# Masked copies in blocks of 32 keys by 32 queries in a chunked gated linear scan: one instruction for all partitions instead of four

## The chip, the cores and the metric

The kernel runs on one core of one Trainium2 chip. The metric is the device time of one execution in microseconds (us). Engines are named as in the profile: PE is TensorE (PEld its weight loads), DVE is VectorE, ACT is ScalarE, POOL is GpSimd, SP issues DMAs. Each engine takes its own instructions strictly in order and waits on semaphores for the others.

## The reference

One inference step of a decoder layer on 256 prompt tokens and 8 x 4 sample tokens, width 2048: a SwiGLU block, a mixer, a second SwiGLU block, each with RMSNorms around it. The mixer projects the tokens, runs two groups of gated recurrences (GLA: 4 heads with value width 256; HGRN2: 8 heads with value width 128; key width 128 in both), normalises and gates their outputs and projects back.

```python
def gated_linear_scan(q, k, v, log_a, s0):
    # S_t = diag(exp(log_a_t)) S_{t-1} + k_t^T v_t ;  o_t = q_t S_t
    ...
    def step(s, inp):
        qi, ki, vi, gi = inp                      # one chunk of c tokens
        cum = jnp.cumsum(gi, axis=2)
        diff = cum[:, :, :, None, :] - cum[:, :, None, :, :]
        decay = jnp.where(causal, jnp.exp(jnp.where(causal, diff, 0.0)), 0.0)
        scores = jnp.sum(qi[:, :, :, None, :] * ki[:, :, None, :, :] * decay, axis=-1)
        o = (jnp.einsum('bhts,bhsv->bhtv', scores, vi)
             + jnp.einsum('bhtd,bhdv->bhtv', qi * jnp.exp(cum), s))
        last = cum[:, :, -1:, :]
        s_new = (jnp.exp(last[:, :, 0, :])[..., None] * s
                 + jnp.einsum('bhsd,bhsv->bhdv', ki * jnp.exp(last - cum), vi))
        return s_new, o
```

What matters here are the `scores`: for each query token t and each key token s not after it, the sum over 128 features of q_t times k_s times the decay from s to t. For s = t there is no decay, and the score is the plain sum of q_t k_t.

## The kernel before

**Products.** Nearly all time goes to dense products. An activation tile holds 128 features by 288 tokens (256 prompt, 32 sample). Weights arrive as float32 tiles of 128x1024 and are split into a high part `wh` (ACT, L96) and a low part `wl` (DVE, L97). `block` multiplies each with the activations' two parts in three products per 128x128 piece, on L548 (high by high), L549 (low activations by high weights) and L550 (high activations by low weights). Four split weight tiles are held ahead. The names of the products are `gate`, `up`, `out` (the SwiGLU blocks), `qk`, `v`, `hfq`, `hi`, `gate` and `mo` (the mixer).

**Scans.** Six scans, one per pair of heads (two GLA, then four HGRN), run while `block` works on the next projection: `scan` is a generator, and at each `tick` in `block` it issues its next piece. A scan handles two heads (index a) and two halves of 128 prompt tokens (index i). The scores of one half are gathered in `Dg`, 128 keys by i, a and 128 queries (`Dflat` is the same with i and a joined); those of the sample tokens are in `Ds`. Later `out` multiplies `Dg` and `Ds` with the values.

**Levels.** A pair of tokens s < t belongs to level lv if lv is the highest bit in which they differ: then s lies in the left and t in the right half of a block of 2h tokens, h = 2^lv. At each level `update(lv)` (L1022 and L1025, with the decay products F of L1027) multiplies Q and k with decays, so that one product of k and Q gives that level's scores. In the order of the steps:

- `score01` (L959, L975, L979) gives levels 0 and 1 and s = t; `score23` (L959) levels 2 and 3, from the copies R of L1032, L1037 and L1038; `score(lv)` (L959 for level 4, L1069 for 5 and 6, L1055 for 7) the others.
- For levels 0 to 4 `quarters` computes, for 32 keys each, only the queries of the same 32 tokens: 16 products per call, of 32 keys by 16, 32 or 48 columns. The four groups of 32 keys write the four groups of 32 partitions of PSUM.
- Of these scores only some belong to the level. `put_masked` copies them into the diagonal blocks of `Dg` under a mask `mk` (COPY_PREDICATED on DVE, L968), in four instructions, one for each 32 partitions, since each group of partitions has its own columns in `Dg`. Levels 0 and 1 take eight such instructions, levels 2 and 3 take twelve (level 3 has a near and a far variant). Level 4 needs no mask: ACT copies it in four instructions (L1080). Levels 5 to 7 are copied by ACT (L1086, L1076).
- The sum for s = t is made by a product of the elementwise q k (`own`, in `rp`, L1093, scaled by 128) with a matrix of ones/128. It is split in two reduced-precision parts, `oh` (ACT, L1095) and `ol` (DVE, L1097), and so takes two products of 128x288 (L975). Every partition then holds all sums, and two masked copies with an identity mask (L995) put them on the diagonal of `Dg`; five more (L1001, L1009) fill `Ds`.

The order in which the instructions of each engine stand is not only that of the program: a planner in the framework moves them by its own estimates of when each can start. Each engine then executes its list in that order, whatever the real times are.

**Setup.** `setup` loads the masks as integers into `mi32`, a buffer that `Q` of the first scan uses next (L1096), and POOL casts them to bytes in `mk` (L842).

Of the kernel before, what the change touches and what calls it, by code (L numbers as in the profile page):

```python
# [9 lines left out]
F32 = mybir.dt.float32  # L10
# [115 lines left out]
def trunk_kernel(ctx, tc, x_prompt, x_sample, state_gla, state_hgrn, norm_gains, f1_in, f1_out, f2_in, f2_out,  # L126
# [649 lines left out]
    def mixer(pn, border):  # L776
        with ExitStack() as mx:
# [15 lines left out]
            mk = cst.tile([P, 576], U8, name="mk")  # L793
# [27 lines left out]
            def setup():  # L821
# [20 lines left out]
                G.tensor_copy(mk, mi32)  # L842
# [67 lines left out]
            def scan(d, Vt, V32, Vs, gla, ytile0, s0, sp_out, ss_out):  # L910
# [34 lines left out]
                oh = sp[0].tile([P, T], F32R, name="oh", tag="bd")  # L945
                ol = sp[0].tile([P, T], F32R, name="ol", tag="bd")
# [15 lines left out]
                def put_masked(src, h, m):  # L962

                    for b in range(4):
                        r = slice(b * TS, (b + 1) * TS)
                        dst = Dflat[r, :, r].rearrange("p j (n two k) -> p j n two k", two=2, k=h)[:, :, :, 1, :]
                        mv = mk[r, m * 64 + b * 16:m * 64 + (b + 1) * 16].rearrange("p (n k) -> p n k", k=h)
                        V.copy_predicated(dst, mv.unsqueeze(1).broadcast_to(dst.shape),  # L968
                                          src[r].rearrange("p j (n k) -> p j n k", k=h))

                def score01():

                    ps, po = auxtile("sc01"), auxtile("sc_o")
                    for i, part in enumerate((oh, ol)):
                        PE.matmul(po[:, 0:T], ones[128], part, start=i == 0, stop=i == 1, skip_group_check=True)  # L975
                    quarters(ps, lambda i, a, b: R[:, a, :, i * 64 + b * 16:i * 64 + (b + 1) * 16])
                    for a in range(2):
                        c = T + a * TS
                        PE.matmul(po[0:TS, c:c + TS], k[:, a, TP:T], R[:, a, :, P:P + TS // 2],  # L979
                                  start=False, stop=True, skip_group_check=True)  # L980
                    return ps, po

                def put01(ps, po):
                    def eye(n, m):
                        return mk[0:n, 448:448 + 2 * m].rearrange("p (n two) -> p n two", two=2)[:, :, 0]

                    def odd():
                        for lv in range(2):
                            put_masked(ps[:, 0:P].rearrange("p (j l c) -> p j l c", j=4, l=2)[:, :, lv], 1 << lv, lv)

                    def even():
                        v = Dflat.rearrange("p (i a) (n two) -> p i a n two", a=2, two=2)
                        ov = po[:, 0:T].rearrange("p (a c) -> p a c", a=2)
                        for i in range(2):
                            V.copy_predicated(v[:, i, :, :, 0], eye(P, 64).unsqueeze(1).broadcast_to([P, 2, 64]),  # L995
                                              ov[:, :, i * 64:(i + 1) * 64])

                    def sampled():
                        sv = Ds[0:TS].rearrange("p a (n two) -> p a n two", two=2)
                        ov = po[:, 0:T].rearrange("p (a c) -> p a c", a=2)  # L1000
                        V.copy_predicated(sv[:, :, :, 0], eye(TS, 16).unsqueeze(1).broadcast_to([TS, 2, 16]),  # L1001
                                          ov[0:TS, :, P:])
                        for lv in range(2):
                            h = 1 << lv
                            m = mk[:, lv * 64:(lv + 1) * 64]
                            dst = Ds[0:TS].rearrange("p a (n two k) -> p a n two k", two=2, k=h)[:, :, :, 1, :]
                            for a in range(2):
                                c = T + a * TS + lv * 16
                                V.copy_predicated(dst[:, a], m[0:TS, 0:16].rearrange("p (n k) -> p n k", k=h),  # L1009
                                                  po[0:TS, c:c + 16].rearrange("p (n k) -> p n k", k=h))  # L1010

                    return [odd, even, sampled]
# [60 lines left out]
                def put(lv, ps):  # L1073
# [3 lines left out]
                    elif h == 16:  # L1077

                        for b in range(0, P, TS):
                            S.activation(Dflat[b:b + h, :, b + h:b + TS],  # L1080
                                         ps[b:b + h, 0:64].rearrange("p (j c) -> p j c", j=4), AF.Copy)
# [9 lines left out]
                for step in range(LEVELS + 1):  # L1091
                    if step == 0:
                        V.scalar_tensor_tensor(own.unsqueeze(3), halves(q, 1, False), 128.0, halves(k, 1, False),  # L1093
                                               op0=ALU.mult, op1=ALU.mult)
                        S.activation(oh, rp, AF.Copy)  # L1095
                        V.tensor_tensor(Q, q, d["f"], op=ALU.mult)  # L1096
                        V.tensor_tensor(ol, rp, oh.bitcast(F32), op=ALU.subtract)  # L1097
# [28 lines left out]
                    if 3 <= step < LEVELS - 1:  # L1126
# [4 lines left out]
                        elif step == 4:  # L1131
                            sampled()
                            put23(*pss.pop(3))
                        else:
                            put(step - 1, pss.pop(step - 1))
# [387 lines left out]
```

## Time and profile before

| what | value |
|---|---|
| median of 3 runs | 2266.98 us (2266.93 to 2267.67) |
| the profiled execution, its own time | 2267.07 us |
| its span, first to last instruction | 2265.0 us |
| PE, PEld busy in the span | 2244.5 us, 2227.3 us |
| DVE, ACT, POOL busy in the span | 1409.0 us, 1022.7 us, 134.9 us |
| granted TensorE clock | 0.998 |
| scan stage | 923 us to 1246 us of the span |

The page gives each engine's busy share of the span; the windows view gives it for a stretch of time. The view of waits lists who stood idle and whose instruction released it, with total, count and longest in us. The groups show line, engine, operation, output<-inputs, shapes and count, then busy time, mean ns of one, and the idle time before them with its releaser. The timeline lists instructions by start and duration, runs of equal ones merged.

### The profile page before, as it was taken

Reading aid. Unit: us, or ns where it says so; the run is one execution under the profiler, and the core shown is the slowest. Engines: PE = TensorE matmul, PEld = TensorE weight load, DVE = VectorE, ACT = ScalarE, POOL = GpSimd, SP = SyncE. Lnnn points to the kernel's source line nnn. Section 1 sums busy time; section 2 is a strip of 40 time slices with the busy share of each in tenths; the row PEclk is TensorE's granted clock in tenths of the full one; section 3 lists DMA queues with packets and bytes.
Section 4 is the critical chain, followed back from the end, with each engine's and each line's share of the span. In section 5 each row is a group of like instructions: output and inputs, shape, how many; then the busy total and the mean of one; then the engine's idle time right before and its main releaser. Section 6 shows DMA issues by size and latency. Waiting matters only on the chain. (4 is left out here: it accounts for less than half of the span.)

```text
span 2265.0 us, 43259 instructions
## 1 busy us (share of the span) xinstructions
PE 2244.5 (99%) x17760; PEld 2227.3 (98%) x17760; DVE 1409.0 (62%) x2359; ACT 1022.7 (45%) x1581; POOL 134.9 (6%) x241
## 2 busy tenths in 40 slices
PE   9999999999999999999999999999999999999998
PEld 9999999999999999999999999999999999999998
DVE  6545545554555468888889754954555455545546
ACT  6443333333334346555656654644333333333344
POOL 2000000000000001011000000440000000000005
PEclk9999999999999999999999999999999999999999
DMA  6555555555555554566555554565555555555545
GB/s 213 171 165 167 168 167 163 165 167 168 167 164 182 167 168 140 168 187 189 163 167 177 164 186 150 168 190 165 164 167 167 168 164 164 165 168 168 164 164 156
DMA packets 225605, 382.49 MB, mean 169 GB/s; under 512 B 20242, under 2 KB 60224, under 8 KB 225408
## 3 DMA queue, kind: packets, MB, share of 16 engines
q1 hardware_dynamic: 214736, 365.15, 50.6%
q0 software_dynamic: 8496, 14.41, 2.4%
q8 instruction: 139, 2.28, 0.4%
q10 hardware_dynamic: 2176, 0.18, 0.1%
q14 instruction: 58, 0.48, 0.1%
HBM read 363.75 MB, written 11.80 MB: 166 GB/s over the span
## 5 line engine op out<-in xcount | busy, mean ns | idle before, releaser
L97 DVE TENSOR_TENSOR wl<-raw,wh 128x1024 fp32r<-128x1024 f32 (+1 forms) x674 | 821.7, 1220 | 615.3 <-ACT wh L96 612.7
L96 ACT ACTIVATE wh<-raw 128x1024 fp32r<-128x1024 f32 (+1 forms) x674 | 711.5, 1057 | 1018.9 <-PE gate L549 313.7
L548 PE MATMUL gate<-xh,wh 128*128 128x288 f32 x1660 | 488.4, 296 | 0.6 <-ACT xh L254 0.6
L550 PE MATMUL gate<-xh,wl 128*128 128x288 f32 x1660 | 488.5, 295 | 0.4 <-DVE wl L97 0.4
L549 PE MATMUL gate<-xl,wh 128*128 128x288 f32 x1660 | 485.7, 295 | 0.6 <-DVE xl L255 0.6
L549 PE MATMUL out<-hl,wh 128*128 128x288 f32 x1408 | 415.7, 295 | 0.0
L550 PE MATMUL up<-xh,wl 128*128 128x288 f32 x1408 | 415.0, 295 | 0.0
L550 PE MATMUL out<-hh,wl 128*128 128x288 f32 x1408 | 415.0, 295 | 0.0
L548 PE MATMUL up<-xh,wh 128*128 128x288 f32 x1408 | 414.9, 295 | 0.0
L549 PE MATMUL up<-xl,wh 128*128 128x288 f32 x1408 | 414.6, 294 | 0.0
L548 PE MATMUL out<-hh,wh 128*128 128x288 f32 x1408 | 413.7, 294 | 0.0
L548 PEld LDWEIGHTS gate<-xh,wh 128*128 128x128 f32 x1660 | 310.9, 188 | 1.9 <-ACT xh L254 1.0
L550 PEld LDWEIGHTS gate<-xh,wl 128*128 128x128 f32 x1660 | 311.3, 188 | 1.1 <-DVE wl L97 0.8
L549 PEld LDWEIGHTS gate<-xl,wh 128*128 128x128 f32 x1660 | 310.4, 188 | 1.2 <-DVE xl L255 0.8
L550 PEld LDWEIGHTS out<-hh,wl 128*128 128x128 f32 x1408 | 264.7, 188 | 0.0
L548 PEld LDWEIGHTS out<-hh,wh 128*128 128x128 f32 x1408 | 264.6, 188 | 0.0
L549 PEld LDWEIGHTS out<-hl,wh 128*128 128x128 f32 x1408 | 264.4, 188 | 0.0
L548 PEld LDWEIGHTS up<-xh,wh 128*128 128x128 f32 x1408 | 264.1, 188 | 0.3
L549 PEld LDWEIGHTS up<-xl,wh 128*128 128x128 f32 x1408 | 264.2, 188 | 0.1
L550 PEld LDWEIGHTS up<-xh,wl 128*128 128x128 f32 x1408 | 264.2, 188 | 0.0
L706 DVE TENSOR_TENSOR y<-out,y 128x288 f32<-128x288 f32 x288 | 121.2, 452 | 101.3 <-PE out L550 98.3
L548 PE MATMUL hfq<-xh,wh 128*128 128x288 f32 x256 | 77.6, 304 | 0.0
(376 smaller groups left out, 2518.9 us busy)
## 6 DMA issues: line engine op xcount, KB each, us to landing
raw<-in_ffn_w_in_dram SPq DMA_DIRECT2D x351, 512.0 KB, 3.5
raw<-in_ffn_w_out_dram SPq DMA_DIRECT2D x176, 512.0 KB, 3.5
raw<-in_mix_w_in_dram SPq DMA_DIRECT2D x64, 512.0 KB, 3.8
raw<-in_mix_w_in_dram SPq DMA_DIRECT2D x96, 256.0 KB, 3.1
raw<-in_mix_w_out_dram SPq DMA_DIRECT2D x32, 512.0 KB, 3.6
out_dram<-s POOLq DMA_DIRECT2D x32, 256.0 KB, 2.8
s<-in_state_gla_dram SPq DMA_DIRECT2D x16, 256.0 KB, 4.2
s<-in_state_hgrn_dram SPq DMA_DIRECT2D x16, 256.0 KB, 4.2
```

Of the source, the lines that this page charges most:

```text
L96: i1 = self.nc.scalar.activation(h[:, c], raw[:, c], AF.Copy).ins
L97: i2 = self.nc.vector.tensor_tensor(l[:, c], raw[:, c], h[:, c].bitcast(F32), op=ALU.subtract).ins
L548: yield lambda: PE.matmul(dst, w[0][:, c:c + P], parts[0], start=start, stop=False)
L549: yield lambda: PE.matmul(dst, w[0][:, c:c + P], parts[1], start=False, stop=False)
L550: yield lambda: PE.matmul(dst, w[1][:, c:c + P], parts[0], start=False, stop=stop)
L706: V.tensor_tensor(y[k], ps, y[k], op=ALU.add)
```

## The change

The masked copies of levels 0 to 3 no longer write `Dg`. A new tile `Db` holds, for each of the 128 keys, only the 32 queries of its own block, so that all 128 partitions have the same columns, and one COPY_PREDICATED does the work of four. Level 4 goes the same way, on DVE under its mask. A new function `place` copies the four blocks of `Db` to the diagonal of `Dg` on ACT, one step after level 4. The sum for s = t is computed in blocks like the other scores: float32 products with a 128x32 matrix of ones, eight for the prompt and two for the sample, in place of the two of 128x288; `oh` and `ol` go, and the factor 128. `Ds` is filled by three copies instead of five. The masks are cast in eight pieces by POOL, which also fills `Db` with zeros and the ones.

```diff
-            mk = cst.tile([P, 576], U8, name="mk")
+            mk = cst.tile([P, 8, 16], U8, name="mk")
+            one32 = cst.tile([P, TS], F32, name="one32")
+            Db = cst.tile([P, 4, TS], F32, name="Db")
...
-                G.tensor_copy(mk, mi32)
+                G.memset(one32, 1.0)
+                G.memset(Db, 0.0)
+                for b in range(4):
+                    r = slice(b * TS, (b + 1) * TS)
+                    G.tensor_copy(mk[r, 0:7], mi32[r, 0:448].rearrange("p (l c) -> p l c", c=64)[:, :, b * 16:(b + 1) * 16])
+                    G.tensor_copy(mk[r, 7], mi32[r, 448 + b * TS:448 + (b + 1) * TS]
+                                  .rearrange("p (n two) -> p n two", two=2)[:, :, 0])
...
                 def put_masked(src, h, m):
+                    dst = Db.rearrange("p j (n two k) -> p j n two k", two=2, k=h)[:, :, :, 1, :]
+                    mv = mk[:, m, :].rearrange("p (n k) -> p n k", k=h)
+                    V.copy_predicated(dst, mv.unsqueeze(1).broadcast_to(dst.shape),
+                                      src.rearrange("p j (n k) -> p j n k", k=h))
+
+                def place():
                     for b in range(4):
                         r = slice(b * TS, (b + 1) * TS)
-                        dst = Dflat[r, :, r].rearrange("p j (n two k) -> p j n two k", two=2, k=h)[:, :, :, 1, :]
-                        mv = mk[r, m * 64 + b * 16:m * 64 + (b + 1) * 16].rearrange("p (n k) -> p n k", k=h)
-                        V.copy_predicated(dst, mv.unsqueeze(1).broadcast_to(dst.shape),
-                                          src[r].rearrange("p j (n k) -> p j n k", k=h))
+                        S.activation(Dflat[r, :, r], Db[r], AF.Copy)
 
                 def score01():
-                    ps, po = auxtile("sc01"), auxtile("sc_o")
-                    for i, part in enumerate((oh, ol)):
-                        PE.matmul(po[:, 0:T], ones[128], part, start=i == 0, stop=i == 1, skip_group_check=True)
+                    ps = auxtile("sc01")
                     quarters(ps, lambda i, a, b: R[:, a, :, i * 64 + b * 16:i * 64 + (b + 1) * 16])
+                    v = ps[:, P:P + 64].rearrange("p (i a c) -> p i a c", i=2, a=2)
                     for a in range(2):
-                        c = T + a * TS
-                        PE.matmul(po[0:TS, c:c + TS], k[:, a, TP:T], R[:, a, :, P:P + TS // 2],
+                        for b in range(4):
+                            PE.matmul(v[b * TS:(b + 1) * TS, :, a, :], one32,
+                                      own[:, a, 0:P].rearrange("p (i c) -> p i c", i=2)[:, :, b * 16:(b + 1) * 16],
+                                      start=False, stop=True, skip_group_check=True)
+                    for a in range(2):
+                        c = 192 + a * 16
+                        PE.matmul(ps[0:TS, c:c + 16], one32, own[:, a, P:P + 16],
                                   start=False, stop=True, skip_group_check=True)
+                        c = 224 + a * TS
+                        PE.matmul(ps[0:TS, c:c + TS], k[:, a, TP:T], R[:, a, :, P:P + TS // 2],
+                                  start=False, stop=True, skip_group_check=True)
...
+                def put01(ps):
+                    for lv in range(2):
+                        put_masked(ps[:, 0:P].rearrange("p (j l c) -> p j l c", j=4, l=2)[:, :, lv], 1 << lv, lv)
+                    dst = Db.rearrange("p j (n two) -> p j n two", two=2)[:, :, :, 0]
+                    V.copy_predicated(dst, mk[:, 7, :].unsqueeze(1).broadcast_to(dst.shape),
+                                      ps[:, P:P + 64].rearrange("p (j c) -> p j c", j=4))
...
                     elif h == 16:
-                        for b in range(0, P, TS):
-                            S.activation(Dflat[b:b + h, :, b + h:b + TS],
-                                         ps[b:b + h, 0:64].rearrange("p (j c) -> p j c", j=4), AF.Copy)
+                        put_masked(ps[:, 0:64].rearrange("p (j c) -> p j c", j=4), h, lv)
...
-                        V.scalar_tensor_tensor(own.unsqueeze(3), halves(q, 1, False), 128.0, halves(k, 1, False),
-                                               op0=ALU.mult, op1=ALU.mult)
-                        S.activation(oh, rp, AF.Copy)
+                        V.tensor_tensor(own.unsqueeze(3), halves(q, 1, False), halves(k, 1, False), op=ALU.mult)
                         V.tensor_tensor(Q, q, d["f"], op=ALU.mult)
-                        V.tensor_tensor(ol, rp, oh.bitcast(F32), op=ALU.subtract)
...
-                            odd, even, sampled = put01(*pss.pop(1))
-                            odd()
-                            even()
+                            put01(pss[1])
                         elif step == 4:
-                            sampled()
+                            put01_sample(pss.pop(1))
                             put23(*pss.pop(3))
                         else:
                             put(step - 1, pss.pop(step - 1))
+                            if step == 6:
+                                place()
```

`put01_sample` is the former `sampled` with three copies: the diagonal of `Ds`, then one for each of levels 0 and 1, both heads at once.

40 lines of the change are left out of this document (11 added, 29 removed).

## The prediction

> **What bounds the kernel now.** I read the page first, then the windows view cut at the ends of the scan stage, then what TensorE waits for inside that stage, then the timeline around the longest of those waits.
>
> ```profile
> span 2265.0 us, 43259 instructions
> PE 2244.5 (99%) x17760; PEld 2227.3 (98%) x17760; DVE 1409.0 (62%) x2359; ACT 1022.7 (45%) x1581; POOL 134.9 (6%) x241
> DVE  6545545554555468888889754954555455545546
> ```
>
> TensorE is busy 99% of the span, so the time can fall only by its work or by the 20.5 us (2265.0 - 2244.5) in which it stands still. VectorE has spare time as a whole, but slices 16 to 22 of 40, where the scans run, show eight tenths and more.
>
> ```profile
> 0.00:60.00 60.00, 57.29 (x413) 56.06 (x413) 41.53 (x72) 38.24 (x70) 15.38 (x35) 1.00 0.69 212
> 60.00:923.00 863.00, 862.80 (x6506) 861.76 (x6505) 497.03 (x724) 358.52 (x466) 12.88 (x27) 1.00 0.51 165
> 923.00:1246.00 323.00, 315.55 (x3205) 302.84 (x3204) 282.48 (x685) 189.86 (x452) 26.06 (x38) 1.00 0.60 178
> 1246.00:2265.00 1019.00, 1008.85 (x7644) 1006.69 (x7642) 587.94 (x881) 436.06 (x595) 80.58 (x141) 1.00 0.53 167
> ```
>
> The columns are length, then busy PE, PEld, DVE, ACT, POOL. Of TensorE's idle time 7.45 us (323.00 - 315.55) lies in the scan stage; the rest is the start (2.7), the end (10.2) and nearly nothing between. In the scan stage VectorE is busy 282.48 of 323 us, 87%. What ended TensorE's waits there:
>
> ```profile
> PE sc L959 <- DVE k_h L1025: 2.6, 3, 1.2
> PE sc L1069 <- DVE F L1027: 1.6, 2, 1.3
> PE hfq L550 <- DVE wl L97: 1.2, 2, 0.8
> PE sc L959 <- DVE R L1038: 1.0, 2, 0.6
> PE sc L959 <- DVE Dg L968: 0.6, 1, 0.6
> PE sc L1069 <- DVE k_h L1025: 0.3, 1, 0.3
> PE sc L959 <- DVE r L1248: 0.2, 1, 0.2
> ```
>
> Twelve waits, 7.5 us, and VectorE releases every one. Idle time starts only when the modelled tail of the last matmul has ended (matmuls start 0.13 us apart and last 0.29), so up to 0.16 us of each wait is hidden in "busy": 12 x 0.16 is 1.9 us, and removing all twelve is worth 7.5 to 9.4 us. That is the whole prize: nothing else in the change touches the bound. The longest wait shows what VectorE was doing instead:
>
> ```profile
> 1061.52 1.94 DVE L968 COPY_PREDICATED Dg<-mk,sc 32x64 f32<-32x64 uint8 x6
> 1063.94 0.74 DVE L995 COPY_PREDICATED Dg<-mk,sc_o 128x128 f32<-128x128 uint8 x2
> 1066.42 0.21 DVE L1001 COPY_PREDICATED Ds<-mk,sc_o 32x32 f32<-32x32 uint8 x1
> 1066.52 0.47 DVE L1009 COPY_PREDICATED Ds<-mk,sc_o 32x16 f32<-32x16 uint8 x4
> 1066.90 3.02 DVE L968 COPY_PREDICATED Dg<-mk,sc 32x64 f32<-32x64 uint8 x12
> 1069.94 0.43 DVE L1022 TENSOR_TENSOR Q<-Q,F 128x256 f32<-128x256 f32 x1
> 1070.29 0.42 DVE L1025 TENSOR_TENSOR k_h<-k_h,F 128x256 f32<-128x256 f32 x1
> 1070.85 0.33 PE L1069 MATMUL sc<-Q,k_h 128*32 128x32 f32 x16 [1.30 <-DVE F L1027]
> ```
>
> The level-5 scores need the updated Q and k of lines 1022 and 1025. These stood in VectorE's queue behind the twelve copies of levels 2 and 3 (3.02 us), which nobody needed yet. The next weight part, L97, queues in the same way, hence the waits on wl.
>
> **VectorE.** Per scan the old kernel has 20 copies on L968, two on L995, five on L1001 and L1009, and the subtraction L1097.
>
> ```profile
> L97 DVE TENSOR_TENSOR wl<-raw,wh 128x1024 fp32r<-128x1024 f32 x78 | 95.1, 1220 | 11.1 <-ACT wh L96 10.6
> L968 DVE COPY_PREDICATED Dg<-mk,sc 32x64 f32<-32x64 uint8 x120 | 30.4, 254 | 3.4
> L995 DVE COPY_PREDICATED Dg<-mk,sc_o 128x128 f32<-128x128 uint8 x12 | 4.4, 472 | 0.2
> L1009 DVE COPY_PREDICATED Ds<-mk,sc_o 32x16 f32<-32x16 uint8 x24 | 2.9, 180 | 0.0
> L1097 DVE TENSOR_TENSOR ol<-rp,oh 128x288 fp32r<-128x288 f32 x5 | 2.2, 450 | 0.0
> ```
>
> That is 20 x 0.254 = 5.1, plus 0.74 for the pair, 0.57 for the five (1066.42 to 1066.99 above), plus 0.45: 6.9 us. New are seven copies into Db (levels 0 and 1, the diagonal, three for levels 2 and 3, and level 4, which ScalarE did before) and three into Ds. A copy of 64 elements on all 128 partitions is not in the trace. From below: L968's 0.254, since each partition has the same 64 elements; from above: L995's 0.472 for 128 elements on 128 partitions. I take 0.254, the row with the same elements per partition. For Ds, 3 x 0.21 (L1001's size). New total 7 x 0.254 + 0.63 = 2.4 us (3.9 at the upper price). VectorE saves 4.5 us per scan (3.0 at least), 27 us over six scans, and goes from 87% to 79% busy in this stage.
>
> The Trainium skill, page "VectorE: DVE Perf Modes", section "Two Vector instructions with no wait between them", says that an instruction whose operands start in another quadrant of 32 partitions than those before it waits until every earlier one has finished. The trace agrees: the twelve L968, which step through the quadrants, lie 0.25 us apart, a full duration, while the four L1009, all in the first quadrant, lie 0.10 us apart. By this rule the new copies could overlap too, ten of them in some 1.2 us where nothing waits, and the sum below would be about 0.2 us better.
>
> What this does to the waits: ahead of the level-4 update stand, of a scan's copies, six L968 (1.94), the L995 pair (0.74) and the subtraction (0.45), and in their place comes one diagonal copy (0.25): that update can be 2.9 us earlier. Ahead of level 5 the twelve become three, 3.02 to 0.76, another 2.3: 5.1 us in all. Ahead of the level-2 and level-3 scores (R L1038) little moves: 0.45 us, and in the fifth scan, by the order of the instructions, four copies.
>
> The changed program's instruction order has the scores of the first two scans (GLA) where they were. In the four HGRN scans the planner, which also sees the shorter queue, puts them earlier: level 4 by 0, 14, 10 and 4 matmuls, level 5 by 2, 17, 14 and 14. At 0.133 us each that asks VectorE for at most 1.9 us at level 4 and 2.3 us at level 5. The largest demand is the fourth scan's level 4, 1.9 plus its wait of at most 1.2: 3.1 against 2.9, so 0.2 us stays there. Level 5 has 5.1 against at most 2.3 plus 1.3. Of the R waits (1.0) I leave 0.4. VectorE then meets ScalarE more often (L97 waits 10.6 us for wh already); for a new wait on wl or an update I put 0.4. So 1.0 us of the 7.5 stays, and **6.5 us** go. The hidden 0 to 1.9 us I keep for the low end.
>
> **TensorE's own work.** One scan's level-0/1 scores in the timeline:
>
> ```profile
> 926.44 0.30 PE L975 MATMUL sc_o<-oh,ones 128*128 128x288 f32 x1
> 926.58 0.29 PE L975 MATMUL sc_o<-ol,ones 128*128 128x288 f32 x1
> 926.79 0.46 PE L959 MATMUL sc<-R,k_g 128*32 128x32 f32 x32
> 927.07 0.29 PE L979 MATMUL sc_o<-R,k_g 128*32 128x32 f32 x4
> 927.29 0.40 PE L548 MATMUL qk<-xh,wh 128*128 128x288 f32 x1
> ```
>
> The removed pair starts 0.14 us apart: 0.27 us. Sixteen quarter matmuls are 32 records and take 0.28 us (926.79 to 927.07), 0.0088 per record, because four column groups run side by side. The eight new ones of the diagonal have the same form: 16 records, 0.14. The two new sample ones join L979's, which all use one column group: 4 records at most (927.29 - 927.07)/4 = 0.055 each, 0.22; at 0.0088, 0.04. So 0.18 to 0.36 for 0.27, -0.1 to +0.1 per scan, within 0.6 us for all six; I take 0. The Trainium skill, page "FP8 and Floating Point Precision", section "TensorE Precision Notes", speaks against this trade: a true fp32 product takes four passes through the array, reduced precision one. The trace shows two records per fp32 matmul. Were the new ones twice as dear as the rows say, the estimate would be 0.26 us more per scan, 1.5 us in all, and the result 2262.1.
>
> **ScalarE and GpSimd.**
>
> ```profile
> L1080 ACT ACTIVATE Dg<-sc 16x64 f32<-16x64 f32 x24 | 5.2, 215 | 9.2 <-DVE Dg L968 6.0 <-PE hfq L549 2.7
> L896 ACT ACTIVATE vs<-tp_v 32x128 f32<-32x128 f32 x13 | 3.3, 252 | 0.0
> L1095 ACT ACTIVATE oh<-rp 128x288 fp32r<-128x288 f32 x5 | 2.2, 434 | 1.1 <-DVE rp L1093 1.1
> ACT Dg L1080 <- DVE Dg L968: 6.0, 3, 3.5
> 910.38 0.66 POOL L842 CAST mk<-mi 128x576 uint8<-128x576 int32 x1
> 920.96 0.76 DVE L1096 TENSOR_TENSOR Q<-q_g,f_g 128x576 f32<-128x576 f32 x1 [0.26 <-ACT f_g L159]
> ```
>
> Four copies of 16x64 (0.86) become four placements of 32x128 (4 x 0.252 = 1.0), and L1095 (0.43) goes: 0.3 us less per scan on an engine that is 59% busy there (189.86 of 323). The placements wait for VectorE's level-4 copy, and behind them in ScalarE's queue stand the wh splits (L96). The old ones waited likewise, 6.0 us in total for L968; the new ones come a step later and find a shorter queue. I cost them at nothing; the cover is that lag, and the second rival prices its loss. On GpSimd one mask cast becomes eight, with two memsets more: at 0.66 at most each, 9 x 0.66 = 6 us, more likely about 2. The mask's buffer is next written by Q at 920.96, 9.9 us after the cast's end at 911.04: nobody waits. If that cover were gone, the first scan would start later by the excess, once. No DMA is added; the planner only swaps one state load with weight loads on SP's queue.
>
> **The sum.** The profiled execution took 2267.07 us, 2.1 us above its span, and 0.09 above the median of 2266.98. 2267.07 - 6.5 + 0 = **2260.6**. About 0.2%, 4.5 us, is what a measurement of this kernel can tell from no change.
>
> **Rivals.** *The planner spends the relief.* The earlier scores of the HGRN scans wait again. For it: they stand up to 2.3 us earlier. Against: the update is up to 5.1 us earlier. If the waits of L959 and L1069 on k_h (2.6 and 0.3), those on wl (1.2) and half of R's stay, 4.6 of 7.5, the gain is 2.9: 2264.2. If VectorE spends all of it waiting for wh, the change does nothing: 2267.
>
> *ScalarE becomes the late one*, on the slower side. The placements wait for VectorE, wh waits behind them, wl behind wh, and TensorE for wl. Old waits of 6.0 us at L1080 fell in three places, and beside them TensorE lost 1.2 us on wl. If each of six scans lost those 1.2 us and the score waits stayed because VectorE stands behind wh, the time is 2267.07 + 6 x 1.2 - 1.2 = 2273.1. It decides once the placements wait longer than the weights are split ahead, which is about 2 us where the old 6.0 in three waits just reached TensorE. Against it: level 4's copy is now one instruction, and ScalarE has 41% to spare.
>
> **Numbers.** The forecast has 0.62, with its own range of 2258.0 (2267.07 - 9.1, nearly all twelve waits with their hidden part) to 2262.5. The first rival with the case of no effect has 0.27, ScalarE's 0.11. The range 2258.0 to 2268.0 takes in the first rival and the bounds on TensorE's work, and leaves out the slower rival and a little below. Faster 0.62, same 0.27, slower 0.11.
>
> **What would show it.** Right: in the scan stage TensorE's idle time falls from 7.45 us to about 1, VectorE's busy time from 282 to about 255, L968's row is gone for 42 copies of 128x64 near 0.25 us, and the waits of "sc" on k_h and F are gone. Wrong: "sc" still waits for k_h at the new places (first rival); ACT waits for Db with wh behind it, and "hfq" or "gate" for wl (second); the diagonal's sixteen records take over 0.3 us; or copies on 128 partitions near 0.47 us.

## The result and the profile after

| | median | lowest to highest | ratio to before, 95% interval |
|---|---|---|---|
| before, 5 runs | 2267.12 us | 2266.93 to 2268.95 | |
| changed kernel, 5 runs | 2257.19 us | 2256.56 to 2258.92 | 0.9956 (0.9943 to 0.997) |
| changed kernel, second set, 5 runs | 2259.59 us | 2258.04 to 2259.91 | 0.9965 (0.9951 to 0.9979) |

The change makes the kernel faster by 9.9 us in the first comparison and by 7.9 us in the second, where before had 2267.52. The forecast was a gain of 6.5 us, 2260.6, with a range of 2258.0 to 2268.0: the first median lies 0.8 us below the range, the second inside it.

The page of the changed kernel (profiled execution: 2256.56 us), in the lines that were shown of before:

```profile
span 2254.8 us, 43365 instructions
PE 2242.7 (99%) x17868; PEld 2227.0 (99%) x17868; DVE 1379.7 (61%) x2251; ACT 1021.4 (45%) x1575; POOL 136.1 (6%) x250
DVE  7545545554565468788888755954555455545646
```

TensorE's busy time is 1.8 us less than before (2244.5), the span 10.2 us less: most of the time came out of recorded standing still. The windows view for the scan stage, and all of TensorE's waits in it:

```profile
923.00:1246.00 323.00, 322.73 (x3398) 311.03 (x3397) 261.17 (x595) 197.67 (x466) 26.00 (x38) 1.00 0.61 181
PE sc L967 <- ACT R L958: 0.3, 1, 0.3
```

Idle time fell from 7.45 us to 0.27. None of the waits on VectorE is left; the one that stays is on ScalarE's copy R. VectorE's new copies, then ScalarE's placements, as groups of the scan stage (line, engine, operation, output<-inputs, shapes, count, busy time, mean ns of one, idle time before), and the two waits that the prediction had named as dangerous, taken from 915 to 1255 us:

```profile
L974 DVE COPY_PREDICATED Db<-mk,sc 128x64 f32<-128x64 uint8 x36 | 8.9, 246 | 0.2
L1017 DVE COPY_PREDICATED Ds<-mk,sc 32x32 f32<-32x32 uint8 x12 | 2.5, 212 | 0.1
L1005 DVE COPY_PREDICATED Db<-mk,sc 128x64 f32<-128x64 uint8 x6 | 1.8, 296 | 0.0
L1010 DVE COPY_PREDICATED Ds<-mk,sc 32x32 f32<-32x32 uint8 x6 | 1.3, 209 | 0.0
L980 ACT ACTIVATE Dg<-Db 32x128 f32<-32x128 f32 x24 | 7.4, 307 | 6.9 <-DVE Db L974 6.7
ACT Dg L980 <- DVE Db L974: 6.7, 4, 2.1
DVE wl L97 <- ACT wh L96: 19.3, 23, 2.2
```

**How the kernels are compared below.** The large products (L548 to L550) are the same in every kernel and run in almost the same order, so their start times in two traces can be laid side by side. Number 6650 starts before the scans (898.1 us in before), number 8700 behind them (1255.9 us). The *scan gain* of a kernel is how much less time it needs from the one to the other than before does. These differences are worked out from the start times in the traces and stand in no row of a view. For the changed kernel the scan gain is 9.05 us. In stretches that begin at product 6816 and end at numbers 7200, 7536, 7790, 8190, 8460 and 8700 it collects 0.7, 0.0, 2.1, 3.9, 0.7 and 1.6 us. The other large part of the 10.5 us between the two profiled executions (2267.07 and 2256.56) is the start: product 100 comes 1.57 us earlier (23.23 us instead of 24.80). Between the scans and the last large product no stretch differs by more than 0.2 us, and what follows that product takes 0.3 us longer.

### The profile page after: what moved, and what is told of

Its sections match the earlier page's. It is cut to its first block, busy times and chain, and to the rows that moved or that the text cites. A ratio compares the mean times of both kernels' runs of the same rounds, so it can differ in the third digit from the quotient of the medians.

```text
span 2254.8 us, 43365 instructions
## 1 busy us (share of the span) xinstructions
PE 2242.7 (99%) x17868; PEld 2227.0 (99%) x17868; DVE 1379.7 (61%) x2251; ACT 1021.4 (45%) x1575; POOL 136.1 (6%) x250
## 4 chain that ended last, share of the span: by engine, by line
PE 97%; DVE 2%; ACT 0%; issue 0%; DMA 0%; DVEq 0%; POOL 0%; ACTq 0%; SPq 0%; POOLq 0%
PE gate L548 10%; PE gate L550 9%; PE gate L549 9%; PE up L550 8%; PE up L548 8%; PE up L549 8%; PE out L549 8%; PE out L550 8%; PE out L548 8%; PE mo L550 2%; PE mo L548 2%; PE mo L549 2%; PE hfq L548 1%; PE hfq L550 1%; PE hfq L549 1%; PE qk L548 1%
## 5 line engine op out<-in xcount | busy, mean ns | idle before, releaser
L97 DVE TENSOR_TENSOR wl<-raw,wh 128x1024 fp32r<-128x1024 f32 (+1 forms) x674 | 821.8, 1220 | 620.2 <-ACT wh L96 617.2
L548 PE MATMUL gate<-xh,wh 128*128 128x288 f32 x1660 | 488.9, 296 | 0.0
L550 PE MATMUL gate<-xh,wl 128*128 128x288 f32 x1660 | 488.7, 295 | 0.0
L550 PE MATMUL up<-xh,wl 128*128 128x288 f32 x1408 | 415.1, 295 | 0.0
L550 PE MATMUL out<-hh,wl 128*128 128x288 f32 x1408 | 415.0, 295 | 0.0
L548 PE MATMUL up<-xh,wh 128*128 128x288 f32 x1408 | 414.8, 295 | 0.1
L548 PE MATMUL out<-hh,wh 128*128 128x288 f32 x1408 | 413.7, 294 | 0.0
L548 PEld LDWEIGHTS gate<-xh,wh 128*128 128x128 f32 x1660 | 310.9, 188 | 1.2 <-DVE u L626 0.2
L550 PEld LDWEIGHTS gate<-xh,wl 128*128 128x128 f32 x1660 | 311.5, 188 | 0.4 <-DVE wl L97 0.4
L550 PEld LDWEIGHTS out<-hh,wl 128*128 128x128 f32 x1408 | 264.7, 188 | 0.0
L548 PEld LDWEIGHTS out<-hh,wh 128*128 128x128 f32 x1408 | 264.6, 188 | 0.0
L548 PEld LDWEIGHTS up<-xh,wh 128*128 128x128 f32 x1408 | 264.1, 188 | 0.5 <-ACT g L618 0.3
L550 PEld LDWEIGHTS up<-xh,wl 128*128 128x128 f32 x1408 | 264.2, 188 | 0.0
L548 PE MATMUL hfq<-xh,wh 128*128 128x288 f32 x256 | 77.9, 305 | 0.0
```

The lines of the kernel that those rows point to most:

```text
L97: i2 = self.nc.vector.tensor_tensor(l[:, c], raw[:, c], h[:, c].bitcast(F32), op=ALU.subtract).ins
L548: yield lambda: PE.matmul(dst, w[0][:, c:c + P], parts[0], start=start, stop=False)
L550: yield lambda: PE.matmul(dst, w[1][:, c:c + P], parts[0], start=False, stop=stop)
```

## The experiments

**The two halves of the change.** *Sum alone*: before, with the sum in quarters, four diagonal copies into `Dg` (each group of 32 partitions has its own columns) and `Ds` in three copies.

```diff
-                        for i in range(2):
-                            V.copy_predicated(v[:, i, :, :, 0], eye(P, 64).unsqueeze(1).broadcast_to([P, 2, 64]),
-                                              ov[:, :, i * 64:(i + 1) * 64])
+                        for b in range(4):
+                            r = slice(b * TS, (b + 1) * TS)
+                            dst = Dflat[r, :, r].rearrange("p j (n two) -> p j n two", two=2)[:, :, :, 0]
+                            V.copy_predicated(dst, eye(r, 16).unsqueeze(1).broadcast_to(dst.shape),
+                                              ps[r, P:P + 64].rearrange("p (j c) -> p j c", j=4))
```

> The kernel before with only the sum for s = t changed: float32 products in quarters, no oh and ol, the diagonal copied by four masked copies of 32x64 and the sample scores by three copies; the masked copies of levels 0 to 3 stay four instructions each, level 4 stays on ScalarE. Queue theory (the gain comes from the copies that stood in VectorE's queue ahead of the updates of Q and k): VectorE loses only about 0.7 us per scan, so 2265 to 2267 us, and TensorE still waits 5 to 7.5 us in the scan stage. Rival (the gain comes from the sum: the two wide products, their split and their PSUM tile are gone): about 2259 us, and the waits go.

Measured: 2272.51 us, ratio 1.0022 (1.0013 to 1.0031): slower, and outside what either theory had given. Scan gain -4.3 us. Its waits of TensorE in the scan stage, the three largest:

```profile
PE sc L959 <- DVE k_h L1030: 4.2, 3, 1.8
PE sc L1074 <- DVE F L1032: 2.1, 2, 1.6
PE sc L959 <- DVE Dg L968: 1.8, 2, 1.3
```

VectorE's timeline in the first scan, before:

```profile
932.12 0.43 DVE L1022 TENSOR_TENSOR Q<-Q,F 128x256 f32<-128x256 f32 x1
932.47 1.22 DVE L97 TENSOR_TENSOR wl<-raw,wh 128x1024 fp32r<-128x1024 f32 x1
933.72 0.74 DVE L995 COPY_PREDICATED Dg<-mk,sc_o 128x128 f32<-128x128 uint8 x2
```

and with the sum alone:

```profile
931.74 1.23 DVE L97 TENSOR_TENSOR wl<-raw,wh 128x1024 fp32r<-128x1024 f32 x1
933.00 1.23 DVE L1002 COPY_PREDICATED Dg<-mk,sc 32x64 f32<-32x64 uint8 x4
934.23 0.43 DVE L1027 TENSOR_TENSOR Q<-Q,F 128x256 f32<-128x256 f32 x1
```

Four copies that step through the groups of partitions take 1.23 us, the former pair 0.74, and in this kernel's list the update of Q stands behind them and behind a weight part. VectorE was not relieved of 0.7 us per scan, as I had expected: between products 6650 and 8700, the same work in both kernels, it is busy 312.92 us against 310.19 in before. How the 4.3 us divide between the step and the moved order was not separated.

*Blocks alone*: the changed kernel with the old sum (`oh`, `ol`, two products of 128x288); its diagonal is copied into `Db` by four instructions, since every partition holds all sums.

```diff
+                oh = sp[0].tile([P, T], F32R, name="oh", tag="bd")
+                ol = sp[0].tile([P, T], F32R, name="ol", tag="bd")
...
-                    V.copy_predicated(dst, mk[:, 7, :].unsqueeze(1).broadcast_to(dst.shape),
-                                      ps[:, P:P + 64].rearrange("p (j c) -> p j c", j=4))
+                    for b in range(4):
+                        r = slice(b * TS, (b + 1) * TS)
+                        dst = Db[r].rearrange("p (i a) (n two) -> p i a n two", a=2, two=2)[:, :, :, :, 0]
+                        src = ov[r, :, 0:P].rearrange("p a (i c) -> p i a c", i=2)[:, :, :, b * 16:(b + 1) * 16]
+                        V.copy_predicated(dst, mk[r, 7, :].unsqueeze(1).unsqueeze(1).broadcast_to(dst.shape), src)
```

> The changed kernel with the old sum for s = t: oh and ol and two products of 128x288, the diagonal brought into Db by four masked copies; everything else as changed. Queue theory: 2257.5 to 2260 us, TensorE waits under 1.5 us in the scan stage. Rival (the sum carries the gain): about 2265 us.

Measured: 2258.78 us, ratio 0.996 (0.9948 to 0.9973); scan gain 7.9 us. Nearly the whole gain is the blocks; the new sum adds 1.1 us to it, and costs 4.3 us without them.

**Is it the step through the partitions, or the number of copies?** *Four copies*: the changed kernel, but levels 0 to 3 go into `Db` by four instructions, one for each 32 partitions, as they went into `Dg` before.

```diff
+                    parts = [slice(0, P)] if h == 16 else [slice(b * TS, (b + 1) * TS) for b in range(4)]
+                    for r in parts:
+                        dst = Db[r].rearrange("p j (n two k) -> p j n two k", two=2, k=h)[:, :, :, 1, :]
```

> The changed kernel with only one thing undone: the copies of levels 0 to 3 into Db are again four instructions each, one per 32 partitions; Db, place, level 4 and the sum stay as changed. Queue theory: 2263 to 2266 us, with TensorE's waits for k_h and F back at 4 to 7 us. Rival (the sum, or ScalarE no longer waiting for VectorE's copies at level 4): 2257 to 2259 us.

Measured: 2268.54 us, ratio 1.0002 (0.9994 to 1.0011): the whole gain is gone, more than the 2263 to 2266 us that I expected; scan gain -0.2 us. Its group of copies, one run of them in VectorE's timeline, and TensorE's three largest waits:

```profile
L976 DVE COPY_PREDICATED Db<-mk,sc 32x64 f32<-32x64 uint8 x120 | 30.4, 253 | 3.3
1067.94 2.79 DVE L976 COPY_PREDICATED Db<-mk,sc 32x64 f32<-32x64 uint8 x11
PE sc L967 <- DVE k_h L1032: 2.7, 4, 0.9
PE hi L548 <- DVE z L1362: 1.5, 1, 1.5
PE sc L1076 <- DVE F L1034: 1.0, 2, 0.8
```

Eleven copies take 2.79 us, 0.25 apart, as before; the waits on k_h and F are back.

*Split by columns*: the same number of instructions, but each of all 128 partitions and a quarter of the columns, so that all of them start at partition 0.

```diff
+                    parts = [slice(0, 4)] if h == 16 else [slice(j, j + 1) for j in range(4)]
+                    for j in parts:
+                        dst = Db[:, j].rearrange("p j (n two k) -> p j n two k", two=2, k=h)[:, :, :, 1, :]
```

> The changed kernel, but each masked copy of levels 0 to 3 is split into four by columns: one for each of the four groups of 32 queries, each on all 128 partitions and starting at partition 0. As many instructions as in the run with four copies per 32 partitions, which lost the whole gain, and the same elements, but no step from one group of 32 partitions to the next. If that step is what spaces the copies 0.25 to 0.33 us apart (quadrant theory), these lie about 0.1 us apart, 20 of them cost some 2 us per scan instead of 5, and the time is 2257 to 2261 us. If the number of instructions is what counts, 2265 to 2269 us.

Measured: 2258.62 us, ratio 0.9965 (0.9953 to 0.9977); scan gain 8.94 us, and 0.3 us of waits in the stage.

```profile
L976 DVE COPY_PREDICATED Db<-mk,sc 128x16 f32<-128x16 uint8 x120 | 12.5, 170 | 0.1
```

120 copies, as many as in the row above, occupy VectorE for 12.5 us instead of 30.4, though 120 x 0.170 is 20.4: they overlap and start about 0.10 us apart. Between the two kernels the planner also moved instructions of all three engines, TensorE's among them, so a cleaner pair follows below.

*Four copies at levels 2 and 3 only.*

```diff
+                    parts = [slice(b * TS, (b + 1) * TS) for b in range(4)] if h in (4, 8) else [slice(0, P)]
```

> The changed kernel with four copies per 32 partitions at levels 2 and 3 only (twelve in place of three per scan, 2.3 us more in VectorE's queue ahead of the level-5 update); levels 0 and 1 stay one instruction each. Queue theory with the prediction's split (level 5 and wl behind the twelve: 1.6, 0.3 and 1.2 us of the waits): 2259 to 2263 us, and the waits that come back are those for F (level 5) and wl, not those for k_h at level 4. Rival (all of the copies' load counts alike): half of the way back and in all waits alike, about 2263 us with k_h at level 4 among them.

Measured: 2261.72 us, ratio 0.9976 (0.9967 to 0.9985); scan gain 6.0 us, so these twelve copies per scan cost 3.0 of the 9.05 us. If the parts add up, the eight of levels 0 and 1 cost the larger part; they were not run alone. The waits on F and wl that I expected back did not come; the two longest:

```profile
PE hi L548 <- DVE z L1362: 1.1, 1, 1.1
PE sc L1076 <- DVE k_h L1032: 0.7, 2, 0.5
```

The second is for k_h at level 5; the first is a product of the projection `hi` that waits for VectorE's `z`, a victim that the prediction did not name.

**Does it matter where the copies stand?** *Late copies*: the changed kernel with 20 additional copies per scan into a scratch tile, behind the last level, where no score of the scan needs VectorE any more.

```diff
+                    for m, h in ((0, 1), (1, 2)) if a == 0 else ((2, 4), (3, 8), (6, 8)):
+                        for b in range(4):
+                            r = slice(b * TS, (b + 1) * TS)
+                            dst = Dx[r].rearrange("p j (n two k) -> p j n two k", two=2, k=h)[:, :, :, 1, :]
+                            ...
+                            V.copy_predicated(dst, mv.unsqueeze(1).broadcast_to(dst.shape),
+                                              kd[r, 0, 0:64].rearrange("p (j n k) -> p j n k", j=4, k=h))
```

> The changed kernel with VectorE's load put back, but in another place: 20 masked copies of 32x64 per scan, one per 32 partitions as before the change, into a scratch tile that nobody reads, issued with the key copies after the last level. Nothing is left out. Queue theory (only copies that stand ahead of the updates of Q and k cost time): 2257 to 2260 us, VectorE some 30 us busier than in the changed kernel. Rival (VectorE's total load in the scan stage sets the time): 2264 us or more.

Measured: 2268.17 us, ratio 1.0003 (0.9994 to 1.0013); scan gain 0.2 us. My theory that only the copies ahead of the updates cost time falls: as many copies behind the last level cost as much. TensorE waits elsewhere then; the group of the additional copies (those between 915 and 1255 us) and two of the waits:

```profile
L1158 DVE COPY_PREDICATED Dx<-mk,kd 32x64 f32<-32x64 uint8 x106 | 27.0, 255 | 3.3 <-ACT kd L1150 0.6
PE sn L1210 <- DVE s L1213: 1.6, 1, 1.6
PE sn L1210 <- DVE bd L1165: 0.8, 1, 0.8
```

`sn` is the new state; its pieces bd and s now stood behind the additional copies. All its waits in the stage come to 5.4 us, and after the one of 1.6 us the granted clock was 0.70 from 1210 to 1215 us, with large products 0.24 us apart instead of 0.13; so part of the 8.9 us that are lost against the changed kernel was lost by the clock. *Late copies by columns* puts as many copies at the same place, of 128x16 and all from partition 0:

```diff
+                        for j in range(4):
+                            dst = Dx[:, j].rearrange("p (n two k) -> p n two k", two=2, k=h)[:, :, 1, :]
+                            mv = mk[:, m, :].rearrange("p (n k) -> p n k", k=h)
+                            V.copy_predicated(dst, mv, kd[:, 0, j * 16:(j + 1) * 16].rearrange("p (n k) -> p n k", k=h))
```

> The late copies inside the scans again, as many as in the run before (20 per scan, at the same place), but split by columns: each 128x16, all starting at partition 0. If the step from one group of 32 partitions to the next makes a copy dear (0.25 us apart), these lie about 0.1 us apart, take 2 us per scan in place of 5, and at most 2 to 4 of the 9 us are lost: 2258 to 2262 us. If the number of instructions or their place is what counts, 2266 to 2268 us again.

Measured: 2259.34 us, ratio 0.9959 (0.9944 to 0.9974), and in the scans the same times as the changed kernel (scan gain 9.03 us). The group, again between 915 and 1255 us:

```profile
L1157 DVE COPY_PREDICATED Dx<-mk,kd 128x16 f32<-128x16 uint8 x108 | 10.8, 181 | 0.9 <-ACT kd L1150 0.6
```

**Outside the scans.** *Copies after the scans*: the changed kernel with 8 additional stepping copies behind each of the 16 tiles of the output projection `mo`, where VectorE has idle time.

```diff
+                for m, h in ((2, 4), (3, 8)):
+                    for b in range(4):
+                        r = slice(b * TS, (b + 1) * TS)
+                        dst = Dx[r].rearrange("p j (n two k) -> p j n two k", two=2, k=h)[:, :, :, 1, :]
+                        mv = mk[r, m, :].rearrange("p (n k) -> p n k", k=h)
+                        V.copy_predicated(dst, mv.unsqueeze(1).broadcast_to(dst.shape),
+                                          y[k][r, 0:64].rearrange("p (j n k) -> p j n k", j=4, k=h))
```

> The changed kernel with 128 masked copies of 32x64, one per 32 partitions, into a scratch tile that nobody reads, spread over the output projection behind the scans (eight after each of its 16 tiles); nothing is left out. The run with late copies inside the scans came back to the old time, so a copy costs there too, wherever it stands. If what counts is that VectorE has hardly a gap in the scan stage, the same load in a stage where it has gaps costs nothing: 2257 to 2260 us. Rival (VectorE's total work, or the copies themselves whatever the stage): 2265 us or more.

Measured: 2270.46 us, ratio 1.0014 (1.0004 to 1.0024), a miss: spare time in the stage was not enough. The scans keep all but 1.0 us of their gain, 0.8 us more than in the changed kernel are lost along the projection, and 11.3 us where it ends. TensorE's wait there, VectorE's timeline ahead of it, and windows of 5 us:

```profile
L1465 DVE COPY_PREDICATED Dx<-mk,y 32x64 f32<-32x64 uint8 x128 | 28.5, 222 | 3.4
PE postm L403 <- DVE acc L396: 6.5, 1, 6.5
1403.71 1.93 DVE L1465 COPY_PREDICATED Dx<-mk,y 32x64 f32<-32x64 uint8 x8
1405.65 0.46 DVE L394 TENSOR_TENSOR sq<-y 128x288 f32<-128x288 f32 x1
1406.03 1.22 DVE L97 TENSOR_TENSOR wl<-raw,wh 128x1024 fp32r<-128x1024 f32 x1
1407.16 0.45 DVE L396 TENSOR_TENSOR acc<-acc,sq 128x288 f32<-128x288 f32 x1
1410.00:1415.00 5.00, 5.00 (x22) 5.00 (x23) 2.19 (x6) 0.80 (x2) 0.00 (x0) 0.50 0.06 23
```

The mean of the last norm (`postm`) needs the sum of squares `acc`, and this stood behind the copies of the last tiles. Two controls followed. *First tiles*: the copies behind the first ten tiles only.

```diff
-                for m, h in ((2, 4), (3, 8)):
+                for m, h in ((2, 4), (3, 8)) if k < 10 else ():
```

> As the kernel with 128 copies of 32x64 in quadrant steps after the scans, but only behind the first 10 of the 16 tiles of the output projection: 80 copies, some 18 to 20 us of VectorE time, none ahead of the last sums of squares. Theory (stepping copies cost only where TensorE waits for what stands behind them in VectorE's queue): 2257 to 2260 us, TensorE's wait at the post-norm (6.5 us there) back below 1 us, scan stage as after. Rival (VectorE work costs TensorE time in proportion wherever it runs): 10/16 of the 12 us lost, 2264 to 2267.

Measured: 2259.61 us, ratio 0.9966 (0.9953 to 0.9979). The copies still take VectorE's time, and TensorE's only wait behind the scans is another norm's:

```profile
L1465 DVE COPY_PREDICATED Dx<-mk,y 32x64 f32<-32x64 uint8 x80 | 17.9, 223 | 2.1
PE postf L403 <- DVE sq L394: 0.2, 1, 0.2
```

18 us of additional VectorE work cost 1.4 us here against the changed kernel, by the start times of the products, and not 10/16 of 11.3. They lie at four steps between products of `mo`, three of them behind ScalarE's `y` with 0.11 us of idle time each, too short for the view of waits. (In the scans 1.0 us is lost, as in the kernel with all 128, for the most part at one wait on R; a few of VectorE's instructions stand in another order there.) *Columns after the scans*: all 128 copies, but by columns from partition 0, with the edit of the late copies by columns.

> The same 128 additional copies at all 16 tiles of the output projection, but as 128x16 copies that all start at partition 0. If holding between groups of 32 partitions made the queue long: the wait at the post-norm falls from 6.5 us to below 2 and the time is 2257 to 2262. If the number of copies alone did it: as the stepping ones, 2268 to 2272. A copy of 16 elements takes 0.17 us by itself (0.22 for the stepping ones), so without overlap the queue would be a quarter shorter and the time near 2266.

Measured: 2260.46 us, ratio 0.9963 (0.9949 to 0.9978).

```profile
L1464 DVE COPY_PREDICATED Dx<-mk,y 128x16 f32<-128x16 uint8 x128 | 12.4, 175 | 0.8 <-ACT y L1459 0.8
PE postm L403 <- DVE acc L396: 0.4, 1, 0.4
```

This is the cleaner pair: TensorE's list is the same in both kernels, VectorE's differs in the place of one weight part and ScalarE's in that of one squaring. The weight part does bear on the wait: it is the L97 at 1406.03 above, which stands ahead of the last `acc` with the stepping copies and behind it here, and accounts for 1.1 us (from 1406.03 to 1407.16). The number of copies is equal, those that step occupy 28.5 us and the others 12.4, and the waits are 6.5 and 0.4 us; so some 5 of the 6.1 us between them are left for the step.

**How much is chance.** *Before again* and *the changed kernel again*, without an edit.

> The kernel before once more, for its start: in the first profile TensorE reached its 100th large product 1.7 us later than in the changed kernel's profile, although both run the same instructions until then. If that is chance in the arrival of the first loads, this profile's start lies anywhere between the two; if it belongs to the kernel, it is again 1.5 us later than the changed kernel's. Time 2267 us either way.

> The changed kernel once more: its start and its time beside the others on the same chip. If the 1.7 us by which its first profile was ahead after the start were chance, this start lies between 0 and 1.7 us behind that one; the scan stage again 9 us shorter than before, 2257 to 2258.5 us.

Measured: 2267.27 us, ratio 1.0001 (0.9992 to 1.001), and 2259.59 us. The scan gain of the second profile of the changed kernel is 9.06 us, against 9.05 in the first. The start is not so steady, and here my expectation missed: product 100 starts at 25.82 us instead of 23.23, 2.6 us later where I had allowed 1.7, and the time lies above 2258.5. Three of TensorE's waits in the first 60 us of the second profile of the changed kernel:

```profile
PE gate L548 <- ACT xh L254: 1.6, 1, 1.6
PE warm L297 <- POOL onesD L228: 1.1, 1, 1.1
PE gate L549 <- DVE xl L255: 0.6, 1, 0.6
```

In its first profile only the wait of `warm` is there; before had 0.6, 0.6 and 0.4 us on xh, xl and wl beside it. Product 6650, up to which no scan has run, starts at 899.98 us instead of 896.59: another 0.8 us went at one wait of `out` for VectorE's u near 728 us. Two executions of the same kernel thus differ by 3.4 us ahead of the scans, 2.6 of it from the start. What decides there was not followed.

## Why the prediction missed

**The bound and the mechanism: right.** The twelve waits in the scan stage went, and they are 8.2 of the 9.05 us, as worked out below. The waits on k_h, F, wl and Dg are gone; four stepping copies in place of one bring those on k_h, F and wl back.

**The residual of 1.0 us: too large.** I kept 0.2 us for the fourth scan, 0.4 for R and 0.4 for new waits; the stage shows 0.27, so idle time fell by 7.18 us (7.45 - 0.27) where the sum had 6.5.

**The size of the sum: this is the step that failed.** The sum counted recorded idle time alone. It kept what the waits cost beyond that at 0, though I had worked out up to 1.9 us for it, and it took TensorE's own work as 0. The scan gain is 9.05 us, 1.9 more than the fall of idle time. This is not the hidden part come in full, though the number is the same. My 0.16 us per wait took 0.13 us for the step to the next product if nothing waits. That holds between large products; from a large product to one of scores the trace of before shows more, without and with a wait (the scores behind the third row start at 1070.85, in a row of the prediction):

```profile
1065.26 0.29 PE L550 MATMUL hfq<-xh,wl 128*128 128x288 f32 x1
1065.48 0.45 PE L959 MATMUL sc<-Q,k_h 128*32 128x16 f32 x32
1069.27 0.29 PE L549 MATMUL hfq<-xl,wh 128*128 128x288 f32 x1
```

Without a wait the step is 0.22 us. The waiting one is 1.58, so 1.36 are lost, and 1.30 are recorded as idle. Over all twelve waits (ten in front of scores, two between large products) the steps lose 8.50 us and 7.45 are recorded: the hidden part is 1.05 us. The wait that stays after the change loses 0.33. So the waits give 8.2 us (8.50 - 0.33) of the scan gain.

The other 0.9 us are TensorE's own. With the losses at waits taken off, by the start times, the way from product 6650 to 8700 takes 349.30 us before, 348.99 with the blocks alone and 348.42 in the changed kernel. In before, small products interrupt the large ones 106 times there, in the changed kernel 100 times. What else is in the 0.9 us was not separated.

With these sizes the sum is 7.2 + 1.0 + 0.9 = 9.1 us, so 2258.0, which is the low end of the range.

**The start: not in the sum.** It took the first result over that end: product 100 came 1.57 us earlier than in before. This part is chance, for the start differs by 2.6 us between two profiles of the changed kernel with the same scan gain. The second set, 2.4 us slower in the median, lies inside the range, by luck: the sum for the scans, 6.5 us where 9.05 came, is too small in both.

**VectorE's relief: the durations right, the occupation better.** I took 7 copies at 0.254 and 3 at 0.21 us per scan, 2.4 us; the four rows give 8.9 + 1.8 + 2.5 + 1.3 = 14.5 us for six scans. The upper price of 0.472 did not come. But successive copies overlap, in the changed kernel's timeline:

```profile
1061.38 0.21 DVE L1017 COPY_PREDICATED Ds<-mk,sc 32x32 f32<-32x32 uint8 x1
1061.48 0.21 DVE L974 COPY_PREDICATED Db<-mk,sc 128x64 f32<-128x64 uint8 x1
1061.62 0.22 DVE L1017 COPY_PREDICATED Ds<-mk,sc 32x32 f32<-32x32 uint8 x1
1061.73 0.22 DVE L974 COPY_PREDICATED Db<-mk,sc 128x64 f32<-128x64 uint8 x1
```

They start 0.10 to 0.14 us apart, the large ones with 64 elements on each of 128 partitions. The rule of the Trainium skill, page "VectorE: DVE Perf Modes", section "Two Vector instructions with no wait between them", that an instruction waits for all earlier ones when its operands start in another quadrant of partitions, was weighed at 0.2 us in the prediction. The runs agree with the rule and give it far more weight: of two kernels with equally many copies, the one that steps loses 9.1 us in the scans (-0.2 against 8.94). VectorE's busy time in the stage fell to 261.17 us, not to 255, since the same 323 us now hold more of the work that follows. Between products 6650 and 8700 it fell by 28.8 us (310.19 to 281.43), close to the 27 of the prediction.

**The products of the sum for s = t: 0 in the first scan, as taken.** They stand in the changed kernel between these large products:

```profile
924.76 0.29 PE L550 MATMUL qk<-xh,wl 128*128 128x288 f32 x1
925.25 0.33 PE L989 MATMUL sc<-rp,one 128*32 128x32 f32 x14
925.39 0.21 PE L989 MATMUL sc<-rp,one 128*32 128x32 f32 x2
925.74 0.40 PE L548 MATMUL qk<-xh,wh 128*128 128x288 f32 x1
```

From the last large product to the next it is 0.98 us (924.76 to 925.74); in the timeline of before it is also 0.98 (from the product that starts at 926.31, ahead of the rows shown, to 927.29). The 16 records of the diagonal run from 925.25 to about 925.4, the 0.14 us of the prediction. The doubled price that it put beside the Trainium skill's page "FP8 and Floating Point Precision" (2262.1) did not show. That page states the four passes; the one pass of a reduced-precision product is the prediction's reading of it. Over six scans TensorE's own work gave 0.9 us, as said above, and the prediction's bound of 0.6 us did not cover that.

**ScalarE and GpSimd: covered, as taken.** The placements take 0.307 us each instead of 0.252 and wait 6.7 us for `Db`, in four places, longest 2.1; no wait of TensorE on wl or wh followed. So the second rival did not come. Its deciding point of 2 us was just reached, without effect. GpSimd's eight casts end at 911.17 us, and VectorE's Q (L1096) waits 0.3 us for f_g, not for them.

**The planner's earlier scores: harmless.** The first rival's waits on k_h and wl are absent. Its weight of 0.27, and with it the high end of the range, came from the fear that what is asked earlier would not be ready; the updates were ready.

## What to carry to other kernels

A loop over groups of 32 partitions with one small VectorE instruction each was dear here because none of them overlapped the next: lay the data out so that one instruction, or several that start at the same partition, cover all 128. Price a chain of small instructions by the distance of their starts in the timeline and not by their durations. Look for what stands behind them in the queue of an engine that seems to have time: 28 us of copies cost 11 us where a norm's sum stood behind them, and 18 us of them cost 1.4 us where it did not. Price a wait by the step from start to start against the same step without a wait, and not by the recorded idle time.

## What the runs showed of the hardware

- VectorE's copies of 128x64 and 32x32 that start at the same partition last 0.21 to 0.30 us and start 0.10 to 0.14 us apart where none waits; those of 32x64 that step through the groups of 32 last 0.22 to 0.26 us and start about 0.25 us apart.
- The wait of 6.5 us for `acc`, at a place where TensorE has nothing else, cost nearly double. After it the granted clock was 0.50 in the window from 1410 to 1415 us, and of the 11.3 us lost there the 4.8 beyond the wait go with this clock. The Trainium skill, page "TensorE: Matmul & The Clock Gate", Part 1, has the clock at half after an idle window of about 3.4 us, which agrees with this wait.
- Shorter waits are not always safe, and no length that is safe was found. With the sum alone, waits of up to 1.8 us left the granted clock of the scan stage at 1.00. With the late copies, a clock of 0.70 (1210 to 1215 us) followed a wait of 1.6 us. With 128 copies by columns, the wait for `acc` was 0.4 us, and a window behind it had a clock of 0.75:

```profile
1405.00:1410.00 5.00, 5.00 (x31) 5.00 (x30) 3.53 (x10) 1.80 (x4) 0.00 (x0) 0.75 0.06 24
```

2.1 us were lost there in that profile; what lowered the clock was not tested.
